# Block norms with an integer guess and Newton steps, and one memory pool per operand of gate and up, in a one-core decoder step

## The chip, the cores and the metric

The kernel is written for one NeuronCore of a Trainium2 chip. A core has five engines with an in-order instruction queue each: the matrix engine (PE, whose weight loads are listed apart as PEld), VectorE (DVE), ScalarE (ACT), GpSimd (POOL) and SyncE (SP), which here only issues DMAs. They share an on-chip memory of 128 partitions (SBUF), and matrix results go to a small accumulator memory (PSUM). The metric is the device time of one launch in microseconds; lower is better. Before the change it was 1488.21 us, the median of three runs (1481.99, 1488.21 and 1488.89).

## What is computed

One layer of a decoder with hybrid attention is applied to 1024 prompt tokens and 64 sample tokens (8 sequences of 8), 1088 columns in all, with shared weights and a width of 1024, followed by a last norm:

```python
def rms_norm(x, g):
    y = x * lax.rsqrt(jnp.mean(x * x, axis=-1, keepdims=True) + EPS)
    return y * g

h = rms_norm(x, norm_mix)
z = h @ w_in                        # queries, three K/V pairs, gates, pooling channels
o_att = nsa(...)                    # compressed, selected and window branch, gated per head
o_pool, _ = pool_mix(...)           # trailing means over 2/4/8/16 positions, small matrix each
x = x + jnp.concatenate([o_att, o_pool], axis=-1) @ w_out
h = rms_norm(x, norm_ffn)           # the "block norms" of this document
gate, up = jnp.split(h @ w_ffn_in, 2, axis=-1)      # 2 x 2816 columns
x = x + (silu(gate) * up) @ w_ffn_out
y = rms_norm(x, norm_final)
```

The new K/V rows, windows and pooling states are outputs too. A norm needs one reciprocal square root for each token: one number per partition when a tile holds 128 tokens.

## The kernel before

All matrix products are made from 32-bit numbers split in two parts of lower precision, hi and lo (`split`, lines 162 to 164): ACT casts the source to hi, DVE subtracts hi from the source to get lo. Three products (hi by hi, hi by lo, lo by hi) take the place of one. So nearly every operand of PE passes through one ACT and one DVE instruction first.

The work goes through these stages, in the order of the program.

- *First norm and projections* (0 to about 250 us). `norm1` takes x in three chunks of 384, 384 and 320 tokens. It transposes x (line 280), scales the copy by the norm's weights into `h1h` and `h1l` (lines 283 and 284), sums squares on ACT (line 293), calls `rstd_ops`, and spreads the root over the partitions with another transpose (line 300). The product with `w_in` runs on the unscaled columns, and its result is multiplied by the root (line 305).
- *Attention* (to about 698 us). Eight query blocks by two K/V groups by two head pairs give 32 units. The score products of the next unit (lines 918 and 919), their biases and minima on DVE (lines 924 and 939), the exponentials on ACT (line 949), the scaling by gates on POOL (line 997), the transposes of the probabilities (line 1007, copied out and split at 1015 and 1016) and the products with V (lines 1031 and 1032) are woven together by a stream written out by hand. Into it `fill` (called once for each transposed pair of blocks) threads a second, slower stream: first the sample tokens and the pooling half of the output projection, then `att_out`.
- *`att_out`* handles nine tiles of tokens in the order in which attention finishes them (0, 1, 2, 7, the samples, 6, 5, 4, 3): the attention half of the output projection (lines 1193 to 1195), the sum into x (line 1267), the square and its sum on ACT (line 1281), `rstd_ops`, the scaling of x into h (line 1283), and in `h_out` the transposes of h (line 1298) and the multiplication by the norm's weights (line 1299). All tiles but the last go to DRAM (`hdA`, `hdB`); the last one is written straight into the input blocks of the next stage.
- *Gate and up* (about 719 to 1190 us). The 1024 rows and 1088 columns of h form four blocks, hA[0], hA[1], hB[0] and hB[1], each 128 x 4 x 544 numbers. One product of two-by-two blocks is made with seven products instead of eight, named P1 to P7. Their right-hand operands are: P1 is hA[0], P2 is hA[1], P3 is hB[1], and P4 to P7 are sums and differences of blocks, made by `combos` (lines 1315 to 1327) in two pieces, columns 0 to 416 and then 416 to 544; only the second piece has columns of the last attention tile. Each operand is split into `bh…` and `bl…`, 128 x 2176 numbers each. The weights get the same treatment (`side_w`), four products ahead. `chains` runs the products in the order that `sequence` writes out: P1 and P2 of the first unit come first, then P1 of the second, then those that need the combinations. The program calls for the splits of P1 and P2 and two products, then for the rest of the last norm (`self.tail`), then for `combos`.
- *Down projection, last norm* (to the end), with a square root on ACT for each last norm (line 245).

Two things set the order in which instructions stand in an engine's queue. A planner places them at build time: by the order of the program, by when their inputs are expected, and with the threads of `fill` in front. And memory: a tile belongs to a pool, pools are opened and closed like a stack, and the first use of a new pool waits until all tiles under its area have had their last use. The left side of the stack holds constants, then biases (`bias`), then K and V (`kv`), and above them what the threads need, at last `wa`, the pool of `att_out` with its weights, x, h and transposed h. At the entry of gate and up (`ffn`, from line 1466) all but the constants are closed; `fs` (split weights) and then `b2` (the seven operands, some 122 KB of each partition) open over the same area. The input blocks `blk` and the raw weights `wr` lie on the right side.

ACT evaluates functions from a table held in the engine, and an instruction ACT_TABLE_LOAD stands in its queue wherever the next function needs another table. Copies, casts and squares need none of their own here.

Of the kernel before, what the change touches and what calls it, by code (L numbers as in the profile page):

```python
# [11 lines left out]
F32R = mybir.dt.float32r  # L12
I32 = mybir.dt.int32
AF = mybir.ActivationFunctionType
OP = mybir.AluOpType
# [4 lines left out]
D = 1024  # L20
# [11 lines left out]
HT = NT // 2  # L32
# [6 lines left out]
EPS = 1e-6  # L39
# [35 lines left out]
class K:  # L75
# [98 lines left out]
    def consts(self):  # L174
        nc, I, cst = self.nc, self.I, self.cst
        with ExitStack() as s:
            ip = self.pool("ii", 1, stack=s)
            ii = ip.tile([128, 128], I32, name="ii")
            nc.gpsimd.iota(ii, pattern=[[1, 128]], base=0, channel_multiplier=-1)
            self.ident = cst.tile([128, 128], F32, name="ident")  # L180
            nc.vector.tensor_scalar(self.ident, ii, 0.0, None, op0=OP.is_equal)
        self.gm = cst.tile([128, 8], F32, name="gm")
        self.gf = cst.tile([128, 8], F32, name="gf")
        self.rows = cst.tile([128, 64], F32, name="rows")
        self.psc = cst.tile([128, 4], F32, name="psc")
        self.ones = cst.tile([128, 128], F32, name="ones")
        self.ptrow = cst.tile([1, 32], I32, name="ptrow")
        nc.vector.memset(self.ones, 1.0)
        warm = cst.tile([128, 1], F32, name="warm")
        nc.scalar.activation(warm, self.ones[:, 0:1], AF.Ln)  # L190
# [50 lines left out]
    def rstd_ops(self, v, r, t, ss, root=False):  # L241
        nc = self.nc
        nc.vector.tensor_scalar(v, ss, 1.0 / D, EPS, op0=OP.mult, op1=OP.add)
        if root:
            nc.scalar.sqrt(t, v)
            nc.vector.reciprocal(r, t)
        else:
            nc.scalar.activation(t, v, AF.Ln)
            nc.scalar.activation(r, t, AF.Exp, scale=-0.5)
# [3 lines left out]
        nc.vector.tensor_tensor(r, r, t, op=OP.mult)  # L253

# [977 lines left out]
    def att_out(self, pool):  # L1232
# [19 lines left out]
        while todo or nxt:  # L1252
# [29 lines left out]
            self.rstd_ops(v[:rows], r[:rows], t[:rows], ss[:rows])  # L1282
# [186 lines left out]
    def ffn(self, att):  # L1469
        nc, I = self.nc, self.I  # L1470
        with ExitStack() as s:
# [25 lines left out]
            b2p = self.pool("b2", 1, stack=b2)  # L1497
            new = lambda q: (b2p.tile([128, 4, HT], F32R, name="bh" + q), b2p.tile([128, 4, HT], F32R, name="bl" + q))
            B.update({q: new(q) for q in ("P1", "P2", "P5", "P6", "P7", "P4", "P3")})
# [80 lines left out]
    def last_group(self, f0, acts, s):  # L1580
# [72 lines left out]
        self.rstd_ops(v, r, t, ss[:, 0:2], True)  # L1653
# [11 lines left out]
    def final_tile(self, fp, pf, gB, j):  # L1665
# [16 lines left out]
        self.rstd_ops(v[:rows], r[:rows], t[:rows], ss[:rows], True)  # L1682
# [38 lines left out]
```

## Time and profile before

| | |
|---|---|
| runs, median of three | 1488.21 us |
| profiled execution, its own time | 1487.72 us |
| its span | 1485.9 us |
| mean granted clock of PE | 0.964 |
| PE busy | 1374.0 us, 92% |
| DVE busy | 972.8 us, 65% |
| ACT busy | 691.6 us, 47% |
| POOL busy | 199.8 us, 13% |

The profile is one execution, recorded by the hardware. A page gives the busy time of each engine, then the span in 40 equal slices with the busy share in tenths; a line PEclk gives the clock that PE was granted, in tenths of full speed. A busy PE at half clock gets half the work done. Groups of instructions are named by source line, engine, operation and tile, with a count, the busy time and the mean duration in ns; behind them stands how long the engine sat idle just before and what released it, marked "<-". In the timeline each line has a start and a duration in us. Windows list, for a stretch of time, its length, the busy time of PE, PEld, DVE, ACT and POOL with the number of instructions, and then PE's clock, the share of the DMA engines and GB/s. The names there are those of the program without buffer numbers: `bhP` and `blP` are the split operands of gate and up, `blk` their source blocks.

### The profile page before, as it was taken

How to read it: one execution, taken by the hardware profiler on the slowest of the kernel's cores; microseconds unless marked ns; L12 is line 12 of the kernel's file. 1: busy time of each engine (PE TensorE's matmuls, PEld its weight loads, DVE VectorE, ACT ScalarE, POOL GpSimd, SP SyncE). 2: the span in 40 equal slices, each digit the busy share in tenths (PEclk: the TensorE clock that was granted, in tenths of full speed). 3: DMA queues.
4: the chain of work that ended last, by engine and by line, in shares of the span. 5: the costliest groups of instructions: out<-in, count | busy, mean ns of one | idle time of the engine just before them, and what ended most of it. 6: DMA issues, size and time to landing. Idle time of an engine off the chain costs nothing.

```text
span 1485.9 us, 25408 instructions
## 1 busy us (share of the span) xinstructions
PE 1374.0 (92%) x9490; PEld 1275.1 (86%) x9490; DVE 972.8 (65%) x2210; ACT 691.6 (47%) x1545; POOL 199.8 (13%) x338
## 2 busy tenths in 40 slices
PE   6979999999999988987599999999999979999996
PEld 5878999777888867766589999999999979999995
DVE  4655877787676775665775655565555555879558
ACT  7322454766565676865633333333333343525123
POOL 0114223432222221111000000000000010101000
PEclk9989999999999999988789999999999989999998
DMA  6457431543525232311523333332333251536135
GB/s 184 89 136 225 121 95 34 179 144 104 180 90 157 71 114 93 100 57 61 159 58 117 118 104 111 110 102 74 102 104 118 74 209 56 188 99 211 45 106 179
DMA packets 167751, 173.79 MB, mean 117 GB/s; under 512 B 21539, under 2 KB 134787, under 8 KB 166851
## 3 DMA queue, kind: packets, MB, share of 16 engines
q1 hardware_dynamic: 157187, 135.12, 29.8%
q0 software_dynamic: 9392, 35.45, 6.9%
q10 hardware_dynamic: 1048, 1.59, 0.9%
q8 instruction: 75, 1.23, 0.3%
q14 instruction: 49, 0.40, 0.1%
HBM read 113.87 MB, written 58.37 MB: 116 GB/s over the span
## 4 chain that ended last, share of the span: by engine, by line
PE 56%; issue 9%; DVE 8%; ACT 6%; DMA 3%; POOL 1%; SPq 0%; DVEq 0%; POOLq 0%; ACTq 0%
PE pq L1391 34%; PE tp L1007 3%; PE dp L1193 2%; PE O L1031 2%; PE dp L1194 2%; PE dp L1195 2%; PE O L1032 2%; PE S L918 2%; PE S L919 1%; DMA r<-td 1%; ACT ph L1015 1%; DVE pl L1016 1%; DVE blP L164 1%; PE dp L1150 1%; PE dp L1605 1%
## 5 line engine op out<-in xcount | busy, mean ns | idle before, releaser
L1391 PE MATMUL pq<-bhP,sh 128*128 128x272 f32 x1232 | 357.8, 291 | 8.4 <-ACT bhP L163 6.7
L1391 PE MATMUL pq<-blP,sh 128*128 128x272 f32 x1232 | 358.1, 291 | 4.4 <-DVE blP L164 4.4
L1391 PE MATMUL pq<-bhP,sl 128*128 128x272 f32 x1232 | 355.9, 289 | 0.0
L1391 PEld LDWEIGHTS pq<-bhP,sh 128*128 128x128 f32 x1232 | 234.7, 191 | 10.2 <-ACT bhP L163 8.0
L1391 PEld LDWEIGHTS pq<-blP,sh 128*128 128x128 f32 x1232 | 234.3, 190 | 5.4 <-DVE blP L164 5.4
L1391 PEld LDWEIGHTS pq<-bhP,sl 128*128 128x128 f32 x1232 | 234.5, 190 | 0.0
L1391 PE MATMUL pq<-r,sh 128*128 128x272 f32 x1008 | 194.9, 293 | 14.0 <-ACT r L1563 7.4
L163 ACT CAST sh<-ws 128x512 fp32r<-128x512 f32 (+1 forms) x136 | 78.9, 583 | 219.7 <-PE pq L1391 151.9
L1391 PEld LDWEIGHTS pq<-r,sh 128*128 128x128 f32 x1008 | 160.8, 192 | 16.0 <-ACT r L1563 7.6
L164 DVE TENSOR_TENSOR sl<-ws,sh 128x512 fp32r<-128x512 f32 (+1 forms) x136 | 86.7, 640 | 124.8 <-ACT sh L163 124.5
L1391 PE MATMUL pq<-r,sl 128*128 128x272 f32 x504 | 145.3, 289 | 0.0
L1016 DVE TENSOR_TENSOR pl<-tp,ph 128x512 fp32r<-128x512 f32 (+8 forms) x168 | 103.8, 622 | 48.4 <-ACT ph L1015 47.0
L163 ACT CAST sh<-wr 128x512 fp32r<-128x512 f32 (+1 forms) x102 | 59.3, 583 | 154.1 <-PE pq L1391 144.8
L1015 ACT CAST ph<-tp 128x512 fp32r<-128x512 f32 (+8 forms) x168 | 88.6, 533 | 74.8 <-PE tp L1007 66.5
L236 PE MATMUL dp<-h1h,whi 128*128 128x384 f32 (+1 forms) x336 | 113.9, 340 | 3.5 <-DVE ue L305 3.2
L236 PE MATMUL dp<-h1l,whi 128*128 128x384 f32 (+1 forms) x336 | 112.9, 336 | 0.2 <-DVE h1l L284 0.2
L236 PE MATMUL dp<-h1h,wlo 128*128 128x384 f32 (+1 forms) x336 | 112.9, 336 | 0.1
L1560 POOL DMA_DIRECT2D r<-td x21 | 16.0, 764 | 639.8 <-PE pq L1391 638.3
L1391 PEld LDWEIGHTS pq<-r,sl 128*128 128x128 f32 x504 | 96.6, 192 | 0.0
L164 DVE TENSOR_TENSOR sl<-wr,sh 128x512 fp32r<-128x512 f32 (+1 forms) x102 | 64.9, 637 | 39.3 <-ACT sh L163 39.2
L1031 PE MATMUL O<-ph,vn 128*128 128x256 f32 x264 | 81.7, 323 | 5.1 <-ACT ph L1015 3.8
L997 POOL TENSOR_SCALAR pwin<-pwin,r 128x640 f32<-128x640 f32 (+4 forms) x64 | 42.6, 669 | 316.5 <-DVE r L990 171.3
(348 smaller groups left out, 3108.5 us busy)
## 6 DMA issues: line engine op xcount, KB each, us to landing
wr<-in_w_ffn_in SPq DMA_DIRECT2D x44, 512.0 KB
td<-blk SPq DMA_DIRECT2D x18, 1088.0 KB
r<-td POOLq DMA_DIRECT2D x21, 816.0 KB, 6.7
wr<-in_w_ffn_out SPq DMA_DIRECT2D x48, 192.0 KB
wraw<-in_w_in SPq DMA_DIRECT2D x14, 512.0 KB
x<-in_x_prompt SPq DMA_DIRECT2D x8, 512.0 KB
qi<-qd SPq DMA_DIRECT2D x8, 512.0 KB
op<-odp SPq DMA_DIRECT2D x16, 256.0 KB
```

Source lines behind the costliest of these rows:

```text
L163: nc.scalar.copy(hi, src)
L164: nc.vector.tensor_tensor(lo, src, hi.bitcast(F32), op=OP.subtract)
L236: nc.tensor.matmul(ps, w[:, k, :], x, start=(k == 0 and j == 0), stop=(k == kt - 1 and j == 2))
L918: nc.tensor.matmul(S[:, c0:c0 + n], q, kh[:, k0:k0 + n], start=True, stop=False)
L997: nc.gpsimd.tensor_scalar(t, t, r[:, hh, b:b + 1], 1.0, op0=OP.mult, op1=OP.mult)
L1007: nc.tensor.transpose(tp[:kk, 256 * x + 128 * hh:256 * x + 128 * hh + 128], u["P"][hh, b][:, kb * 128:kb * 128 + kk], self.ident)
L1015: nc.scalar.copy(ph[:kk, a:e], tp[:kk, a:e])
L1016: nc.vector.tensor_tensor(pl[:kk, a:e], tp[:kk, a:e], ph[:kk, a:e].bitcast(F32), op=OP.subtract)
L1031: nc.tensor.matmul(o, vv, ph[:kk, cs], start=(2 * t + x == 0), stop=False)
L1032: nc.tensor.matmul(o, vv, pl[:kk, cs], start=False, stop=(2 * t + x == nb - 1))
L1193: nc.tensor.matmul(ps[:rows], oh[:, k, :rows], wh[:, k, cs], start=(k == 0), stop=False)
L1391: nc.tensor.matmul(ps[:, c, :HQ], w[:, k], x[:, k, cs], start=(fresh and k == 0 and j == 0), stop=(k == kt - 1 and j == 2), skip_group_che ...
```

## The change

There are two parts.

The norms of the first stage keep a routine that uses ACT, but with the square root in place of logarithm and exponential (`rstd_ops`, lines 241 to 253 before). The norms in `att_out` call a new routine, `rstd_bits`. It halves the bit pattern of the number, read as an integer, and subtracts it from a constant, which gives a first guess of the reciprocal root; three Newton steps of three instructions each follow, all on DVE. The warm-up instruction at the start asks for the square root's table instead of the logarithm's.

The seven operands of gate and up get one pool each, `bP1` to `bP3`, opened one after the other in the order P1, P2, P6, P5, P7, P4, P3.

```diff
--- before.py
+++ after.py
@@ -187,7 +187,7 @@
         self.ptrow = cst.tile([1, 32], I32, name="ptrow")
         nc.vector.memset(self.ones, 1.0)
         warm = cst.tile([128, 1], F32, name="warm")
-        nc.scalar.activation(warm, self.ones[:, 0:1], AF.Ln)
+        nc.scalar.sqrt(warm, self.ones[:, 0:1])
 
     def late_consts(self):
         nc, I, bp = self.nc, self.I, self.btp
@@ -238,19 +238,24 @@
                 if cnt % every == 0:
                     yield
 
-    def rstd_ops(self, v, r, t, ss, root=False):
+    def rstd_ops(self, v, r, t, ss):
         nc = self.nc
         nc.vector.tensor_scalar(v, ss, 1.0 / D, EPS, op0=OP.mult, op1=OP.add)
-        if root:
-            nc.scalar.sqrt(t, v)
-            nc.vector.reciprocal(r, t)
-        else:
-            nc.scalar.activation(t, v, AF.Ln)
-            nc.scalar.activation(r, t, AF.Exp, scale=-0.5)
+        nc.scalar.sqrt(t, v)
+        nc.vector.reciprocal(r, t)
         nc.vector.tensor_tensor(t, r, r, op=OP.mult)
         nc.vector.tensor_tensor(t, t, v, op=OP.mult)
         nc.vector.tensor_scalar(t, t, -0.5, 1.5, op0=OP.mult, op1=OP.add)
         nc.vector.tensor_tensor(r, r, t, op=OP.mult)
+
+    def rstd_bits(self, v, r, t, ss):
+        nc = self.nc
+        nc.vector.tensor_scalar(v, ss, 1.0 / D, EPS, op0=OP.mult, op1=OP.add)
+        nc.vector.tensor_scalar(r.bitcast(I32), v.bitcast(I32), -0.5, float(0x5f3759df), op0=OP.mult, op1=OP.add)
+        for _ in range(3):
+            nc.vector.scalar_tensor_tensor(t, r, v, r, op0=OP.mult, op1=OP.mult)
+            nc.vector.tensor_scalar(t, t, -0.5, 1.5, op0=OP.mult, op1=OP.add)
+            nc.vector.tensor_tensor(r, r, t, op=OP.mult)
 
     def x_src(self, j):
         if j < 8:
@@ -1279,7 +1284,7 @@
             r = pool.tile([128, 1], F32, name="r", bufs=2)
             t = pool.tile([128, 1], F32, name="t", bufs=2)
             nc.scalar.activation(h[:rows], x[:rows], AF.Square, accum_out=ss[:rows])
-            self.rstd_ops(v[:rows], r[:rows], t[:rows], ss[:rows])
+            self.rstd_bits(v[:rows], r[:rows], t[:rows], ss[:rows])
             nc.scalar.activation(h[:rows], x[:rows], AF.Copy, scale=r[:rows])
             self.tail = self.h_out(pool, j, rows, h)
             yield
@@ -1494,9 +1499,9 @@
             self.qfree = [0, 1, 2, 3]
             self.fs = self.pool("fs", 1, stack=s)
             b2 = ExitStack()
-            b2p = self.pool("b2", 1, stack=b2)
-            new = lambda q: (b2p.tile([128, 4, HT], F32R, name="bh" + q), b2p.tile([128, 4, HT], F32R, name="bl" + q))
-            B.update({q: new(q) for q in ("P1", "P2", "P5", "P6", "P7", "P4", "P3")})
+            for q in ORDER:
+                bq = self.pool("b" + q, 1, stack=b2)
+                B[q] = (bq.tile([128, 4, HT], F32R, name="bh" + q), bq.tile([128, 4, HT], F32R, name="bl" + q))
             self.ca = self.pool("ca", 1, stack=b2)
             self.split(*B["P1"], hA[0])
             self.split(*B["P2"], hA[1])
@@ -1650,7 +1655,7 @@
                 half(0, (0, 1, 2, 3))
         half(1, (4, 5, 6, 7))
         nc.vector.tensor_tensor(ss[:, 0:2], ss[:, 0:2], ss[:, 2:4], op=OP.add)
-        self.rstd_ops(v, r, t, ss[:, 0:2], True)
+        self.rstd_ops(v, r, t, ss[:, 0:2])
         for j in range(2):
             for hf in range(2):
                 cs = slice(512 * hf, 512 * hf + 512)
@@ -1679,7 +1684,7 @@
         t = fp.tile([128, 1], F32, name="ft", bufs=2)
         nc.vector.tensor_tensor(y[:rows], ps[:rows], y[:rows], op=OP.add)
         nc.scalar.activation(sq[:rows], y[:rows], AF.Square, accum_out=ss[:rows])
-        self.rstd_ops(v[:rows], r[:rows], t[:rows], ss[:rows], True)
+        self.rstd_ops(v[:rows], r[:rows], t[:rows], ss[:rows])
         nc.vector.scalar_tensor_tensor(y[:rows], y[:rows], r[:rows], gB[:rows], op0=OP.mult, op1=OP.mult)
         if b < 8:
             nc.sync.dma_start(O["y_prompt"][0, 128 * b:128 * b + 128, :], y[:rows])
```

## The prediction, made before the result was known

> **What bounds the kernel now.** I read the page first: the busy share and the granted clock of the matrix engine, slice by slice (40 slices of 37 us).
>
> ```profile
> span 1485.9 us, 25408 instructions
> ...
> PE   6979999999999988987599999999999979999996
> ...
> PEclk9989999999999999988789999999999989999998
> ```
>
> The matrix engine (PE) sets the time nearly everywhere. Only three places in reach of this change are short of nines or of clock: the start, slices 14 to 18 (attention with the block norms woven in), and slices 18 and 19, where gate and up begin. The loads of ScalarE's function tables come next, from the groups by line with shapes kept apart; columns are count, busy us and mean ns.
>
> ```profile
> L248 ACT ACT_TABLE_LOAD x11 | 14.1, 1283 | 0.2
> ...
> L249 ACT ACT_TABLE_LOAD x9 | 11.5, 1283 | 0.2
> ...
> L949 ACT ACT_TABLE_LOAD x3 | 3.8, 1283 | 0.1
> L190 ACT ACT_TABLE_LOAD x1 | 1.3, 1283 | 0.7 <-PEq L1704 0.7
> ```
>
> Twelve norms (three at the start, nine in attention) each take a logarithm (L248) and an exponential (L249), and each switches tables twice. Three of the second loads show up under the softmax (L949), because a softmax exponential came first. Then eight stretches, one around each of the first eight attention norms: length, busy us of PE, PE's weight loads, DVE, ACT and POOL, and after them PE's granted clock.
>
> ```profile
> 548.00:556.00 8.00, 6.61 (x30) 4.57 (x29) 5.00 (x18) 5.60 (x16) 0.00 (x0) 0.85 0.24 79
> 564.00:576.00 12.00, 9.24 (x47) 7.73 (x46) 5.54 (x20) 6.86 (x15) 1.85 (x3) 0.86 0.33 101
> 584.00:592.00 8.00, 5.35 (x26) 4.39 (x25) 2.36 (x10) 5.29 (x10) 1.85 (x3) 0.79 0.14 33
> 600.00:604.00 4.00, 1.89 (x11) 1.52 (x11) 2.16 (x11) 3.97 (x13) 0.00 (x0) 1.00 0.04 10
> 616.00:620.00 4.00, 2.72 (x17) 1.98 (x17) 3.45 (x12) 3.27 (x10) 0.00 (x0) 1.00 0.11 11
> 632.00:644.00 12.00, 9.84 (x37) 7.03 (x36) 6.50 (x23) 5.42 (x16) 1.63 (x3) 0.72 0.14 44
> 648.00:656.00 8.00, 5.35 (x26) 4.31 (x25) 4.40 (x21) 7.05 (x17) 1.63 (x3) 0.79 0.33 100
> 672.00:684.00 12.00, 8.21 (x41) 6.74 (x39) 5.73 (x29) 9.15 (x22) 3.26 (x6) 0.72 0.12 46
> sum 68.00, PE 49.21 PEld 38.28 DVE 35.14 ACT 46.62 POOL 10.23; mean PE 6.15 PEld 4.78 DVE 4.39 ACT 5.83 POOL 1.28
> ```
>
> PE idles 68.0 − 49.2 = 18.8 us in them, and the clock is low: length times (1 − clock), summed over the eight rows, is 13.0 us. So at most 31.8 us are at stake here. DVE is busy only half of the time (35.1 of 68).
>
> **The change part by part.** *The norms.* One norm before, and the four Newton instructions of another, from the timeline (start, us, engine, line):
>
> ```profile
> 583.77 1.28 ACT L248 ACT_TABLE_LOAD   x1
> ...
> 585.29 1.28 ACT L249 ACT_TABLE_LOAD   x1
> ...
> 586.82 0.16 DVE L250 TENSOR_TENSOR t<-r 128x1 f32<-128x1 f32 x1 [2.85 <-ACT r L249]
> ...
> 588.16 1.16 ACT L1283 ACTIVATE h<-xr,r 128x1024 f32<-128x1024 f32 x1
> ...
> 601.65 0.16 DVE L250 TENSOR_TENSOR t<-r 128x1 f32<-128x1 f32 x1 [1.85 <-ACT r L249]
> ...
> 603.91 0.15 DVE L253 TENSOR_TENSOR r<-r,t 128x1 f32<-128x1 f32 x1
> ```
>
> A load with its activation takes 1.52 us (583.77 to 585.29), so a block norm holds ACT for 3.04 us, and every cast and softmax queued behind it; DVE, whose queue is in order, stops at L250 (2.85 us). The change removes that: 24 loads here (11 + 9 + 3 + 1). It keeps one at the start (the warm-up becomes a square root) and adds one for the first exponential of the gates, so 22 loads of 1.283 us, 28 us of ACT, go. For each of the nine block norms in attention DVE runs eleven dependent instructions in place of five (the three norms at the start are costed below). The integer guess and the scalar_tensor_tensor on 128x1 do not occur before. The nearest rows are the 0.15 and 0.16 us above, and I take 0.2 us with the gap. Back to back that is 2.2 us. But DVE weaves other work between dependent instructions: four of them span 2.4 us in the second group, and eleven at that spacing take some 6.6 us. These are the two ends; six more instructions of 0.2 us for each of eight norms, 10 us of DVE, fit its idle half.
>
> The Trainium skill, "ScalarE: Activation LUTs", "Table sets: the hidden batching unit", says that one set holds logarithm and exponential, so that a pair would need one load; here each pair loads both times, and by the rule there would have been almost nothing to remove. Its section "What ACT_TABLE_LOAD costs" adds 1.38 us of draining to each load; this trace shows 1.52 us with the activation, and 22 loads would be 59 us by the page.
>
> *What of it sets the end.* PE's waits from 540 to 700 (us in total, times, longest):
>
> ```profile
> PE tp L1298 <- ACT h L1283: 6.3, 4, 2.8
> PE tp L1007 <- DVE t L251: 3.5, 1, 3.5
> ```
>
> The transposes of h (L1298) wait 6.3 us for the norm itself. A chain of 11 woven instructions is no shorter than what it replaces, so I leave these 6.3. The other 12.5 us of idle come from work queued behind the loads on ACT, or behind L250 on DVE, as in the second row. What is late next is the chain itself and DVE's evictions: I take two thirds as gained, 8.4 us. The clock:
>
> ```profile
> 588.00:592.00 4.00, 3.94 (x15) 3.26 (x16) 1.25 (x7) 1.33 (x2) 1.85 (x3) 0.60 0.27 66
> 692.00:696.00 4.00, 3.25 (x17) 2.82 (x16) 1.98 (x3) 1.74 (x4) 0.28 (x2) 0.70 0.00 0
> ```
>
> PE is full at clock 0.60 right after the stall of 584 to 588. I let the 13.0 us shrink with the idle, 13.0 x 8.4 / 18.8 = 5.8. Attention: **14.2 us**, ends 0 and 31.8. The second row is a low clock with no norm near, and it speaks against this step (below).
>
> *The start.* PE's waits up to 60 us, one load, one Newton end, the stretch after, and a reciprocal of the softmax:
>
> ```profile
> PE tp L300 <- DVE n1r L253: 2.9, 1, 2.9
> PE tp L280 <- DVE h1l L284: 2.1, 1, 2.1
> ...
> 8.98 1.28 ACT L249 ACT_TABLE_LOAD   x1
> ...
> 29.03 0.16 DVE L253 TENSOR_TENSOR n1r<-n1r,n1t 128x3 f32<-128x3 f32 x1
> ...
> 30.00:35.00 5.00, 5.00 (x22) 3.96 (x20) 2.10 (x5) 3.07 (x7) 0.00 (x0) 0.66 0.02 5
> ...
> L987 DVE RECIPROCAL r<-l 128x3 f32<-128x3 f32 x40 | 6.9, 172 | 2.3 <-ACT pwin L949 1.6
> ```
>
> These three norms do not get the guess: they take one square root on ACT, whose table the warm-up has loaded, and one reciprocal on DVE (0.17 us) in place of logarithm and exponential, and keep the Newton step. The second chunk's transposes of the root (L300) wait 2.9 us for a result that ends at 29.2 behind two loads. Without them, at 1.28 us each, it is there 2.6 us earlier; the activation that goes pays for the reciprocal that comes. So this wait goes but for some 0.3 us, which I neglect; with it half of the 1.7 us (5 x 0.34) that the low clock costs after. The load at 8.98 stands ahead of the first copies of h1, for which PE waits 2.1: 1.28 gained. Together 2.9 + 0.85 + 1.28 = **5.0 us**, ends 0 and 6.7 (2.9 + 2.1 + 1.7). The new exponential load at the gates costs 0 to 1.28; I take 0.6. The final norms keep their square root and their load.
>
> *The pools.* The seven operands of gate and up lay in one pool; now each has its own. The rows where attention ends:
>
> ```profile
> 702.03 0.97 SPq L1482 DMA_DIRECT2D blk<-hdA  x2
> ...
> 710.35 0.15 DVE L243 TENSOR_SCALAR v<-ss 128x1 f32<-128x1 f32 x1 [1.22 <-ACT h L1281]
> 713.37 0.16 DVE L250 TENSOR_TENSOR t<-r 128x1 f32<-128x1 f32 x1 [2.87 <-ACT r L249]
> 716.57 0.69 DVE L1299 TENSOR_TENSOR blk<-tp,gf 128x512 f32<-128x512 f32 x1 [2.46 <-PE tp L1298]
> 717.39 3.91 ACT L163 CAST bhP<-blk 128x2176 fp32r<-128x2176 f32 x2 [1.07 <-PE tp L1298]
> 720.78 4.75 DVE L164 TENSOR_TENSOR blP<-blk,bhP 128x2176 fp32r<-128x2176 f32 x2
> 729.00 0.69 DVE L164 TENSOR_TENSOR sl<-wr,sh 128x512 fp32r<-128x512 f32 x1 [1.67 <-ACT sh L163]
> 729.61 1.88 DVE L1318 TENSOR_TENSOR blk<-blk 128x1664 f32<-128x1664 f32 x1
> ```
>
> The casts of P1 and P2 wait for the last norm's transposes, though their data (hdA, asked for at 702.03) has nothing to do with them. No row shows when it lands; I take it as there by the time x is summed, 709.1. The one pool overlies the tiles that the transposes still read. P1 and P2 in pools at the bottom overlie only the bias and the keys, which are done. From 709.1 (the last sum of x) to the first combination at 729.61 DVE works 12.3 us and idles 1.22 + 2.87 + 2.46 + 1.67 = 8.2. With the 4.75 us of splits free to fill the gaps, and six more small instructions, 13.5 us of work are left; with 2 us of idle it starts 15.5 us after 709.1, at 724.6: **5.0 us**, ends −1.2 (the six instructions, nothing moved, or data that lands late) and 7.0 (no idle). What the casts are moved past: on ACT the last square and scaling (L1281, L1283), which would stand behind casts of 2 us each; on DVE L1267. No store, load or SP entry changes place. The last norm feeds only the second piece of the combinations, so a delay of 2 to 4 us there is covered by the first piece; without that cover it would cost its length.
>
> **The sum.** 14.2 + 5.0 + 5.0 − 0.6 = 23.6. The profiled execution took 1487.7 us (span 1485.9 and 1.8 around it), the runs have a median of 1488.2 (1482.0 to 1488.9). 1487.7 − 23.6 = **1464**.
>
> **The rivals.**
> - *The stalls come back on other engines.* The 6.3 us on h grow as the chain is woven into DVE's evictions. Attention 5, start 3, entry 1.5, less 0.6: 1479. For it: the spacing of 0.6 us above. Against: ACT is free meanwhile. Chance 0.18.
> - *The clock does not follow the stalls.* It is low at 692 to 696 without a norm; if transposes and short waits keep it so, the 5.8 and the start's 0.85 stay: 1470.6, say 1471. Chance 0.12. The Trainium skill, "TensorE: Matmul & The Clock Gate", "HAM oscillation — how this bites in real kernels", puts the limit at gaps of some 3.4 us, and the gap of 584 to 588 is under that; the row of 588 to 592 at 0.60 does not agree.
> - *Nearly everything is gained.* Start 6.7, four fifths of 31.8 = 25.4, entry 7: 1487.7 − 39.1 + 0.6 = 1449. For it: nearly all PE idle of the stretch lies at the norms. Chance 0.16.
> - *Nothing shows*, or the guess and the pools do not do what they say (the casts stay behind the transposes, the stalls keep another cause): 1481 to 1495. Chance 0.07.
> - *Slower: the woven chain.* If a PSUM eviction of 0.62 us stands between every two of the eleven, the chain takes 11 x (0.16 + 0.62) = 8.6 us where loads, activations and Newton took from 583.77 to 588.16, 4.4 us, and later with their own weaving some 6. h is 2.6 us late or more, eight times, 21 to 34 us, and POOL's scaling behind DVE's softmax sums with it; less 9.4 at start and entry: about 1500 to 1512. It decides from some 0.55 us an instruction on. Chance 0.05.
>
> **How the numbers follow.** My forecast has 0.42; its own range is 1456 to 1472. What a measurement of this kernel can tell from no change is about 0.5%, 7.4 us: below 1480.8 is faster. Faster: 0.42 + 0.12 + 0.16 and three quarters of 0.18 = 0.83; within: 0.07 and the rest of the 0.18 = 0.12; slower: 0.05. For 8 in 10 the range takes in the stalls that come back and most of the full gain: 1447 to 1482.
>
> **What would show it.** Two table loads before 540, none from 540 to 730; PE's clock near 0.95 in attention; under 10 us of idle around the norms; the casts of P1 and P2 ahead of the last transposes; combinations starting some 15 us after the last sum of x; gate and up from there on unchanged in length. I am wrong if the eleven instructions take over 6 us from first to last and PE's wait for h grows, or if the first casts still end their wait at L1298.

## The result and the profile after

The changed kernel takes 1446.84 us, the median of four runs (1445.03 to 1448.49), against 1488.55 us for the kernel before, four runs on the same chip (1481.99 to 1489.60). The ratio is 0.9728, with a 95% interval of 0.9703 to 0.9754. The forecast was 1464 us, range 1447 to 1482. The direction was right; the gain is 41.7 us and not 24, and the time lies at the very edge of the range: it is 1447 only when rounded.

From the page of the changed kernel: the span, and by slices the busy share of the matrix engine and its granted clock (40 slices of 36 us).

```profile
span 1446.7 us, 25436 instructions
...
PE   7979999899999989996799999999999989999995
...
PEclk9989999989999999998899999999999999999998
```

Counted from 0, slices 14 to 17 have one eight left of three, and their clock is in the nines. What is left is in slices 18 and 19, the entry of gate and up. ScalarE's table loads, from the groups by line with shapes kept apart:

```profile
L190 ACT ACT_TABLE_LOAD x1 | 1.3, 1283 | 0.7 <-PEq L1709 0.7
L478 ACT ACT_TABLE_LOAD x1 | 1.3, 1283 | 0.0
L1427 ACT ACT_TABLE_LOAD x1 | 1.3, 1283 | 0.0
L244 ACT ACT_TABLE_LOAD x1 | 1.3, 1283 | 0.0
```

Four loads stand where there were 26; none falls in attention. The start: the waits of PE up to 60 us (total, times, longest).

```profile
PE tp L285 <- DMA x<-in_x_prompt: 6.7, 3, 4.5
PE tp L285 <- DVE h1l L289: 0.8, 1, 0.8
```

The window from 30 to 35 us of the same kernel:

```profile
30.00:35.00 5.00, 5.00 (x33) 4.48 (x32) 3.34 (x9) 2.25 (x5) 0.00 (x0) 1.00 0.26 64
```

The wait for the root (2.9 us) is gone, the one for h1 is 0.8 instead of 2.1, and the window from 30 to 35 has the full clock and 33 matrix instructions instead of 22. Attention as a whole, from the first block norm's square to the last product with the values; first the window of the kernel before:

```profile
544.50:698.00 153.50, 131.45 (x710) 105.32 (x709) 96.30 (x320) 106.75 (x262) 29.71 (x51) 0.90 0.24 76
```

Then the same stretch of the changed kernel:

```profile
538.90:665.00 126.10, 120.42 (x711) 96.65 (x710) 101.97 (x369) 84.17 (x230) 30.34 (x51) 0.99 0.29 93
```

And PE's waits in it:

```profile
PE tp L1012 <- DVE pl L1021: 1.9, 3, 1.2
PE O L1036 <- DVE of L1047: 1.2, 1, 1.2
PE S L923 <- ACT psel L954: 1.1, 2, 0.6
PE dp L1198 <- DVE xr L1272: 0.5, 1, 0.5
PE tp L1012 <- POOL pwin L1002: 0.3, 1, 0.3
```

The same work (710 and 711 matrix instructions) takes 27.4 us less. PE's idle time falls from 153.50 − 131.45 = 22.1 us to 5.7, and its busy time falls by 11.0, because the clock rises from 0.90 to 0.99. ACT is busy for 22.6 us less; DVE for 5.7 us more. No wait for h is left.

Where the 39.2 us between the two spans lie, from the times of the same instructions in both traces:

| stretch | before | after | gain |
|---|---|---|---|
| start to the first scaled projection result | 43.5 | 35.6 | 7.9 |
| from there to the first block norm's square | 501.0 | 503.3 | −2.3 |
| attention, to the last product with the values | 153.5 | 126.1 | 27.4 |
| from there to the first product of gate and up | 21.5 | 16.0 | 5.5 |
| gate and up, first to last product | 482.2 | 484.4 | −2.2 |
| from there to the first product of the down projection | 7.9 | 4.7 | 3.2 |
| the rest | 276.3 | 276.6 | −0.3 |

Gate and up ends at 1201.7 us in the kernel before and at 1165.4 in the changed one; the 1190 given above for its end is some 12 us too early. The end of the combinations is the better mark for the entry: from the last product with the values to the last combination it was 52.7 us and is 49.5, a gain of 3.2.

### The profile page after: what moved, and what is told of

Read it like the earlier page. It is cut to its first block, busy times and chain, and to the rows that moved or that the text cites. A ratio compares the mean times of both kernels' runs of the same rounds, so it can differ in the third digit from the quotient of the medians.

```text
span 1446.7 us, 25436 instructions
## 1 busy us (share of the span) xinstructions
PE 1358.5 (94%) x9490; PEld 1263.1 (87%) x9490; DVE 980.2 (68%) x2267; ACT 660.4 (46%) x1502; POOL 200.0 (14%) x338
## 4 chain that ended last, share of the span: by engine, by line
PE 66%; issue 11%; DVE 9%; DMA 5%; ACT 4%; SPq 3%; POOL 1%; DVEq 0%; POOLq 0%; ACTq 0%
PE pq L1396 36%; PE dp L236 6%; PE tp L1012 3%; SPq L1060 3%; PE O L1036 2%; PE dp L1198 2%; PE dp L1200 2%; PE dp L1199 2%; PE O L1037 2%; PE S L923 2%; PE S L924 1%; DVE pl L1021 1%; DMA r<-td 1%; ACT ph L1020 1%; PE dp L1155 1%
```

## The experiments

The theory at test was that of the prediction with its sizes corrected: table loads hold up ACT's queue, PE starves behind it and loses its clock; the start and the pools add gains of their own. The rivals were that DVE's chain or the planner's order, not the loads, sets attention's time, and that the pools do nothing beyond the first casts. All kernels below ran beside the kernel before. The same changed kernel, run again in the second group, took 1445.64 us (1442.33 to 1449.66, ratio 0.9720, interval 0.9692 to 0.9749); single kernels are compared with the 1446 us of these two. The groups ran on different chips, so the ratio to the kernel before on the same chip is given each time.

> The changed kernel once more, on the chip of these runs, as the measure for differences of 3 us: 1445 to 1449.

**The two halves of the change.** The changed kernel with the one pool for the seven operands put back:

```diff
-            for q in ORDER:
-                bq = self.pool("b" + q, 1, stack=b2)
...
+            b2p = self.pool("b2", 1, stack=b2)
...
+            B.update({q: new(q) for q in ("P1", "P2", "P5", "P6", "P7", "P4", "P3")})
```

> The changed kernel with the seven operands of gate and up back in one pool, so the norms' part alone. If the pools gave what the two traces show at the entry of gate and up (3.1 us) and at the start of the down projection (3.3 us), this is 6.4 us above the changed kernel's 1446.8: 1453, and PE's wait there for the down projection's first operand is back at some 7 us. Rival: the pools gave nothing, and the two places moved because the last norm of attention is shorter: 1447 to 1449.

And the kernel before with the seven pools alone (the same edit the other way round):

> The kernel before with one pool per operand of gate and up, its logarithms and exponentials kept, so the pools' part alone. If the two parts add: 1488.5 - 6.4 = 1482, nothing changed before 698 us. If the pools' gain needs the short last norm: 1486 to 1489.

The norms alone took 1452.31 us (ratio 0.9777, 0.9756 to 0.9798): 34.7 us below its kernel before at 1486.97, so the pools bring 5.5 to 6.7 us on top by the medians, and 7 to 8 by the ratios. The pools alone took 1477.03 us (0.9948, 0.9929 to 0.9967), a gain of 7.7 us by the ratio and 9.9 by the medians, and faster than either expectation. From the last product with the values to the last combination it takes 47.2 us (52.7 before), and between the last product of gate and up and the first of the down projection 5.2 us (7.9 before). Its attention has the same order as the kernel before, engine by engine, by names and shapes of the instructions. It has the waits of the kernel before, the same rows with the same numbers for h, t and xr, and yet lasts 146.5 us and not 153.5:

```profile
546.90:693.40 146.50, 124.22 (x710) 100.03 (x710) 96.28 (x320) 106.46 (x262) 29.57 (x51) 0.95 0.25 80
```

Its waits of PE there, the two rows that the prediction showed of the kernel before:

```profile
PE tp L1298 <- ACT h L1283: 6.3, 4, 2.8
PE tp L1007 <- DVE t L251: 3.5, 1, 3.5
```

PE's idle time in it is 22.3 us, as before (22.1). Only the clock differs, 0.95 against 0.90. So some 7 us of attention's 27 vary with the clock of the one execution that was profiled, and idle time is the steadier measure; it is used below. The order of the changed kernel's attention, which six more of the kernels share, shows no such spread: 125.1 to 127.4 us in seven profiles.

**Loads put back, nobody waiting for them.** Logarithm and exponential of a constant for each block norm, written to a tile that nobody reads; the norm itself stays on DVE:

```diff
+            d = pool.tile([128, 2], F32, name="d", bufs=2)
+            nc.scalar.activation(d[:, 0:1], self.ones[:, 0:1], AF.Ln)
+            nc.scalar.activation(d[:, 1:2], self.ones[:, 0:1], AF.Exp, scale=-0.5)
             self.rstd_bits(v[:rows], r[:rows], t[:rows], ss[:rows])
```

> The changed kernel with two short ScalarE instructions added in each of the nine block norms, a logarithm and an exponential of a constant that nobody reads, so that each norm has its two table loads again while the root still comes from VectorE. Theory that the loads hold ScalarE's queue: most of attention's 27.5 us comes back, 1467 to 1474, with 18 loads in attention, PE idle around them and its clock near 0.9 there. Rival, that the norm's own latency or its place in the queues was what PE waited for: below 1453, clock near 0.99.

It took 1471.98 us (0.9907, 0.9884 to 0.9930), 26 us more than the changed kernel. But the planner was free to place instructions without inputs, and put all nine pairs in one row: 18 loads between 508.5 and 536 us. PE's waits from 500 to 540 us:

```profile
PE O L1036 <- ACT ph L1020: 11.7, 1, 11.7
PE tp L1012 <- DVE pl L1021: 9.0, 1, 9.0
```

The window of the same 40 us:

```profile
500.00:540.00 40.00, 18.46 (x107) 15.53 (x107) 12.72 (x44) 37.33 (x68) 3.93 (x6) 0.68 0.11 40
```

This shows directly that loads in ACT's queue stop PE through the casts of the probabilities behind them: 18 x 1.52 = 27.4 us of ACT, 26 us of time. Attention itself, from the first square on, was 126.0 us, as in the changed kernel: the time came out as expected, but not where it was expected. The run doesn't show what the loads cost where the norms stand. So the logarithm was given the sum of squares, and the exponential the logarithm's result:

```diff
...
+            nc.scalar.activation(d[:rows, 0:1], ss[:rows], AF.Ln)
+            nc.scalar.activation(d[:rows, 1:2], d[:rows, 0:1], AF.Exp, scale=-0.5)
             self.rstd_bits(v[:rows], r[:rows], t[:rows], ss[:rows])
```

> The changed kernel with a logarithm of the sum of squares and an exponential of its result added behind each block norm's square, read by nobody. Unlike the constants of the run before, they can not be moved ahead, so the 18 table loads stand where they stood before the change, on ScalarE alone; the root stays on VectorE, which waits for no ScalarE result in it. If it is ScalarE's queue that the loads held: attention again some 18 to 27 us longer than in the changed kernel, 1464 to 1474, with PE's clock near 0.9. If it was VectorE's queue, which stood at the first Newton instruction until the exponential was there: 1447 to 1453.

It took 1468.94 us (0.9863, 0.9830 to 0.9896). Its loads, from the groups by line:

```profile
L1288 ACT ACT_TABLE_LOAD x9 | 11.5, 1283 | 0.2
L1289 ACT ACT_TABLE_LOAD x7 | 9.0, 1283 | 0.1
L954 ACT ACT_TABLE_LOAD x2 | 2.6, 1283 | 0.0
```

The window of its attention:

```profile
537.40:684.70 147.30, 130.19 (x711) 105.39 (x710) 103.11 (x368) 106.91 (x262) 29.58 (x51) 0.90 0.25 79
```

And PE's longest waits in it:

```profile
PE O L1036 <- ACT ph L1020: 4.2, 3, 2.4
PE dp L1198 <- DVE xr L1272: 4.0, 2, 2.9
PE S L923 <- ACT psel L954: 3.5, 4, 1.6
```

With the loads back and nobody using what is computed behind them, the time was 22 to 23 us longer by the medians, attention had 21 of its 27 us back, and PE idled 17.1 us in it. DVE's stop at the first Newton instruction isn't needed for that, since the root here waits for nothing on ACT. That looked like a proof that the loads were the cost.

**The same number of loads, of other functions.** Three more kernels were made to question it. In the first, the block norms take the root on ACT and the reciprocal on DVE, like the norms of the start:

```diff
-            self.rstd_bits(v[:rows], r[:rows], t[:rows], ss[:rows])
+            self.rstd_ops(v[:rows], r[:rows], t[:rows], ss[:rows])
```

> The changed kernel, in which the nine block norms of attention take the square root on ScalarE and the reciprocal on VectorE, as the norms of the start do, so that each norm needs a table load for the root and the next softmax one for the exponential; neither guess nor long Newton chain. Theory A, the loads are what was costly, whoever needs them: like the two unread activations in place (1468.9), within 4 us of it: 1464 to 1473, attention from the first Square to the last product with the values 143 to 151 us. Theory B, the loads cost little where the result is waited for by nobody but the norm, and the shorter VectorE work pays: 1448 to 1458, attention 128 to 136. Theory C, a norm that waits for its own load is worse than one beside it: over 1475, attention over 153.

It took 1452.77 us (0.9770, 0.9742 to 0.9798): only 7 us more than the changed kernel, although each norm loads the root's table and the next softmax the exponential's. The next two kernels ask what made the difference to the 1468.94 us. One puts the second load back into the norm, by an exponential that nobody reads:

```diff
             self.rstd_ops(v[:rows], r[:rows], t[:rows], ss[:rows])
...
+            nc.scalar.activation(d[:rows], v[:rows], AF.Exp, scale=-0.5)
```

> The kernel with the block norms' square root on ScalarE and reciprocal on VectorE, and behind the root an exponential of the mean square into a tile that nobody reads, so that the load of the exponential's table again stands in the norm, ahead of the scaling, and not at the next softmax. As many loads in attention as there (18). Theory A, a second load inside the norm is what made the kernel before and the two unread activations in place so slow (attention 153.5 and 147.3 us against 134.1): 1462 to 1472, attention 143 to 151. Theory B, the place of the second load matters little, and the orders of the work that the planner made are what differs: 1450 to 1458, attention 131 to 138.

The other keeps guess and Newton steps, and beside them takes a root that nobody reads:

```diff
...
+            nc.scalar.sqrt(d[:rows], ss[:rows])
             self.rstd_bits(v[:rows], r[:rows], t[:rows], ss[:rows])
```

> The changed kernel with guess and Newton steps, and beside them a square root of the sum of squares on ScalarE into a tile that nobody reads: one load in the norm, the other at the next softmax exponential, 18 loads in attention, and VectorE's long chain is kept. Theory A, the loads in these places cost the 7 us that the root on ScalarE cost, and VectorE's chain costs nothing: 1450 to 1456, attention 131 to 137. Theory B, loads on ScalarE and the longer chain on VectorE hinder each other, which is why the two unread activations in place cost 23 us: 1462 to 1471, attention 142 to 150.

They took 1453.65 us (0.9818, 0.9775 to 0.9860) and 1454.54 us (0.9800, 0.9765 to 0.9836). Their group's runs of the kernel before had a median of 1484.84, so by the ratios they lie 11 to 14 us above the changed kernel, and by the medians 8 to 9. So DVE's long chain doesn't explain the slow one. The loads of these kernels in the groups by line, and the windows of their attention; first the root on ACT:

```profile
L244 ACT ACT_TABLE_LOAD x10 | 12.8, 1283 | 0.2
L954 ACT ACT_TABLE_LOAD x8 | 10.3, 1283 | 0.1
```

Its window of attention:

```profile
535.60:669.70 134.10, 124.69 (x711) 100.11 (x710) 99.33 (x328) 105.38 (x254) 29.93 (x51) 0.95 0.27 87
```

PE's longest wait in it:

```profile
PE S L923 <- ACT psel L954: 5.8, 3, 3.0
```

Root, then an exponential that nobody reads (the root's row is as above, x10):

```profile
L1289 ACT ACT_TABLE_LOAD x9 | 11.5, 1283 | 0.2
```

Its window of attention:

```profile
537.60:669.70 132.10, 121.22 (x709) 96.61 (x709) 98.10 (x328) 106.28 (x262) 30.12 (x51) 0.99 0.27 89
```

Guess and Newton steps, beside them a root that nobody reads (nine loads at the root, L1288, and eight at the softmax, L954). Its window of attention:

```profile
542.80:678.40 135.60, 125.84 (x710) 101.34 (x709) 105.51 (x368) 105.79 (x254) 29.80 (x51) 0.94 0.27 86
```

ACT is busy for 105 to 107 us in all of them, as in the kernel before, but PE's idle differs. The stretch of attention holds eight norms, and 16 of the 17 or 18 loads; the ninth norm follows at the entry of gate and up.

| kernel | loads in attention | attention, us | PE idle, us | clock |
|---|---|---|---|---|
| before | 16 | 153.5 | 22.1 | 0.90 |
| pools alone | 16 | 146.5 | 22.3 | 0.95 |
| logarithm, then exponential of it, unread | 16 | 147.3 | 17.1 | 0.90 |
| root, then exponential of another tile, unread | 16 | 132.1 | 10.9 | 0.99 |
| root on ACT | 16 | 134.1 | 9.4 | 0.95 |
| root, unread | 16 | 135.6 | 9.8 | 0.94 |
| six Newton steps (next experiment) | 0 | 131.2 | 10.7 | 0.97 |
| changed, two profiles | 0 | 126.1, 125.2 | 5.7, 6.0 | 0.99, 1.00 |

The same 16 loads go with 9.4 us of idle in one kernel and with 22.3 in another. By ACT's timelines the second load of a norm starts 1.5 to 2.0 us after the first in all six kernels (once 4.7, with the unread root): where the norm asks for no exponential, the next softmax does at once. So the kernel that was to put the second load back into the norm hardly moved it, and a second function that reads what the first has written holds ACT no longer than one that doesn't.

What loads as such cost in attention is not isolated either: the kernel with six Newton steps has none there and idles 10.7 us all the same. What ended PE's waits tells more. Waits that end at an exponential or a cast of the probabilities on ACT (`psel`, `pwin`, `ph`) come to 1.1 us in the changed kernel and 0.8 with six Newton steps, to 5.5, 6.3 and 6.6 in the three kernels with a root on ACT, and to 9.5 with the unread logarithm. So some 5 us of idle go with the loads in those three kernels; their attention is 6 to 10 us longer than in the changed kernel, and their time 7 to 14.

The other 6 to 13 us of idle in the slower kernels are not explained by the loads. The kernel before and the one with the pools alone share an order of instructions in attention; each of the other kernels with loads there has an order of its own, since the planner makes it anew, and that order alone may be what differs. A kernel with the order of the kernel before held fixed, and the loads alone taken out, was not tried. What of the 27 us belongs to the loads and what to the order stays open.

**DVE's chain.** Six Newton steps instead of three, nine more instructions a norm:

```diff
-        for _ in range(3):
+        for _ in range(6):
```

> The changed kernel with six Newton steps in place of three: 20 dependent VectorE instructions for each block norm, nine more at 0.2 us, woven into other work, so h comes some 4 to 5 us later. If only ScalarE's queue mattered and the order of the queues takes the longer chain into account: 1446 to 1451. If the chain of the norm is on the path, as the slower rival of the prediction has it: nine norms by 4 to 5 us less what is covered, 1465 to 1490.

It took 1451.51 us (0.9783, 0.9757 to 0.9809), 5 to 6 us more by the medians, 8 to 9 by the ratios, for 81 instructions; this is just above the first of the two expectations. From the end of the square to the start of the scaling a norm now takes 10.0 us in the mean of nine, where it took 6.0 (and 5.7 in the kernel before). PE's wait for it, from the waits from 535.5 to 666.7 us:

```profile
PE tp L1303 <- ACT h L1288: 1.6, 2, 1.3
```

A norm that is 4 us longer makes PE wait 1.6 us for h in all. But that is not its whole price, as the window of attention shows:

```profile
535.50:666.70 131.20, 120.53 (x710) 97.49 (x709) 113.03 (x440) 84.79 (x230) 29.66 (x51) 0.97 0.28 89
```

PE idles 10.7 us, about 5 more than in the changed kernel, and most of the rest ends at other instructions of DVE and POOL. How much of it is the work on DVE, 11 us more, and how much the new order, no run tells apart.

**The start.** The changed kernel with the three norms of the start and the warm-up back on logarithm and exponential:

```diff
-        nc.scalar.sqrt(warm, self.ones[:, 0:1])
+        nc.scalar.activation(warm, self.ones[:, 0:1], AF.Ln)
...
+            nc.scalar.activation(t, v, AF.Ln)
+            nc.scalar.activation(r, t, AF.Exp, scale=-0.5)
...
-            self.rstd_ops(v, r, t, ss)
+            self.rstd_ops(v, r, t, ss, True)
```

> The changed kernel, in which the three norms of the start and the warm-up go back to logarithm and exponential; attention and pools stay as changed. Theory A, the start is a gain of its own that the rest doesn't give back: its traces differ by 7.9 us at the first product of the first stage after the start (43.5 before, 35.6 after), while the stages up to the first block norm gave back 2 us in one profile and nothing in another: 1445.6 + 6 to 8, so 1451 to 1454, with the matrix engine's clock low from 30 to 35 us and a wait of 2 to 3 us on n1r. Theory B, what the start saves is lost again on loads of the first weights, so that only about 2 us of it reach the end: 1446 to 1449, with the first block Square at 537 or earlier although the start is late. My prediction's term was 5.0: 1450.6.

It took 1453.71 us (0.9772, 0.9747 to 0.9797), 7 to 8 us more. The start is a gain of its own, and it reaches the end. In this profile the first scaled result comes at 46.1 us, 10.5 after that of the changed kernel and 2.6 after that of the kernel before, with the clock low for longer. PE's waits up to 60 us:

```profile
PE tp L309 <- DVE n1r L253: 2.9, 1, 2.9
PE tp L289 <- DVE h1l L293: 2.1, 1, 2.1
```

The windows that follow:

```profile
30.00:35.00 5.00, 5.00 (x21) 4.01 (x19) 2.09 (x5) 3.09 (x7) 0.00 (x0) 0.59 0.02 5
35.00:40.00 5.00, 5.00 (x18) 3.12 (x16) 1.10 (x2) 4.23 (x7) 0.00 (x0) 0.50 0.00 0
40.00:45.00 5.00, 5.00 (x20) 5.00 (x20) 2.70 (x7) 1.47 (x3) 0.00 (x0) 0.55 0.33 89
```

**The pools, taken apart.** P1 and P2 with a pool each, the other five in one:

```diff
-            for q in ORDER:
+            for q in ("P1", "P2"):
...
+            bq = self.pool("brest", 1, stack=b2)
+            for q in ORDER[2:]:
```

> The changed kernel with pools of their own for P1 and P2 alone and one pool for the other five operands. Theory that a new pool waits for the whole of every pool that it overlies: the entry of gate and up stays as in the changed kernel (some 49.5 us from the last product of attention to the last combination), but the loads of the down projection's first operands wait for the last product again, 7.9 us from the last product of gate and up to the first of the down projection in place of 4.7: 3 us slower than the changed kernel. Rival, that tiles are released one by one: no difference.

It took 1451.35 us (0.9752, 0.9724 to 0.9780), 4 to 6 us more. The entry was kept (49.5 us from the last product with the values to the last combination), but the gap ahead of the down projection was 8.0 us again. PE's waits there, in the changed kernel first:

```profile
PE pq L1396 <- ACT r L1568: 4.2, 1, 4.2
```

The DMAs of the ring in the same kernel, from POOL's timeline:

```profile
1163.26 5.40 POOL L1565 DMA_DIRECT2D r<-td  x7 [502.84 <-PE pq L1396]
```

The same DMAs in the kernel before:

```profile
1202.49 5.38 POOL L1560 DMA_DIRECT2D r<-td  x7 [510.21 <-PE pq L1391]
```

And PE's wait with the five operands in one pool:

```profile
PE pq L1396 <- ACT r L1571: 7.5, 1, 7.5
```

The down projection reads its ring of operands `r` back from DRAM through seven DMAs on POOL, and the ring overlies the operands of gate and up. In the changed kernel the DMAs are issued at 1163.26, 2 us ahead of the last product of gate and up (1165.4); in the kernel before they were issued at 1202.49, after it (1201.7). If the ring waits for what it overlies, a ring of seven pools should be faster still:

```diff
-            ring = self.pool("ring", 1, stack=s4)
+            ring = [self.pool(f"ring{j}", 1, stack=s4) for j in range(7)]
...
-                r = ring.tile([128, 2, kt, HT], F32R, name=f"r{nr[0] % 7}")
+                r = ring[nr[0] % 7].tile([128, 2, kt, HT], F32R, name=f"r{nr[0] % 7}")
```

> The changed kernel with one pool for each of the seven buffers of the down projection's operands in place of one pool for all seven. By the same theory the first buffers wait only for P1 and P2 of the last unit and not for P4, so their loads are asked for some 10 us earlier and PE's wait of 4.7 us between the two projections falls to 1 or less: 3 to 6 us faster than the changed kernel, 1441 to 1444. Rival, that the loads are held by the DMA queue or by their data: no difference.

It took 1440.62 us (1435.67 to 1442.41, ratio 0.9671, 0.9642 to 0.9700), 5.0 us below the changed kernel on the same chip, and faster than both kernels of this case. The two intervals overlap a little (0.9692 to 0.9700). The DMAs of its ring, from POOL's timeline:

```profile
1139.10 0.84 POOL L1565 DMA_DIRECT2D r<-td  x1 [480.37 <-PE pq L1396]
1148.12 0.76 POOL L1565 DMA_DIRECT2D r<-td  x1 [8.19 <-PE pq L1396]
...
1165.15 0.76 POOL L1565 DMA_DIRECT2D r<-td  x1 [7.25 <-PE pq L1396]
```

They start 24 us earlier and nearly one by one, and PE waits for `r` no more. The planner also moved the work: the first product of the down projection (1156.7) now stands 10.6 us ahead of the last of gate and up, so that the gain is that of the pools and the new order together.

## Why the prediction was right in direction and short in size

- *The loads.* Twenty-two fewer, none in attention: as said. That they hold ACT's queue and what stands behind it is shown by the 18 loads in one row. That they are the main cost of the norms, as the prediction took it, is not shown: in the three kernels with a root on ACT, some 5 us of idle and 7 to 14 us of time go with them, of attention's 20 to 27 us, and each of these kernels has another order too.
- *"A chain of 11 woven instructions is no shorter than what it replaces, so I leave these 6.3."* This step failed. The first half was right: the norm takes 6.0 us where it took 5.7. But PE's wait for h went from 6.3 us to nothing. PE's wait doesn't follow the norm's length: at 10.0 us a norm it is 1.6 us. So the wait can't be the norm's length alone; it came with the order of that kernel's work, and a wait that another order can remove can't be left in the sum on the ground that its chain is as long.
- *"I take two thirds as gained, 8.4 us."* Mis-sized: PE's idle in attention fell by 16.4 us. (Two thirds of 12.5 are 8.3; this changes nothing.)
- *The clock, 5.8 of 13.0 us.* Mis-sized for the same reason: PE's busy time fell by 11.0 us. In proportion to the idle that is gone, as the step had it, some three quarters of the loss would go; the clock of 0.99 says nearly all did. By the two profiles of one order, 0.90 and 0.95, part of this is chance. Attention is 27.4 us by the two profiles, where the term was 14.2 with an upper end of 31.8.
- *The chain's price.* Right. In the norm that follows, the first of attention, the guess starts at 540.84 and the last Newton step at 545.65 (timeline of DVE):

```profile
540.53 0.14 DVE L253 TENSOR_SCALAR v<-ss 128x1 f32<-128x1 f32 x1
...
540.84 0.15 DVE L254 TENSOR_SCALAR r<-v 128x1 int32<-128x1 int32 x1
...
541.24 0.21 DVE L256 SCALAR_TENSOR_TENSOR t<-r,v 128x1 f32<-128x1 f32 x1
...
545.65 0.15 DVE L258 TENSOR_TENSOR r<-r,t 128x1 f32<-128x1 f32 x1
```

  From first to last that is 5.3 us, where 6.6 were reckoned; over the nine norms it is 2.5 to 7.0, and 5.3 in the mean. The unknown instructions took 0.15 and 0.21 us here, where 0.2 was taken with the gap; the second takes 0.28 in the mean of 24 (L256).
- *The start, 5.0 us, upper end 6.7.* Mis-sized: 7.9 by the profiles, 7 to 8 by the kernel that undoes it. The two waits went as said (2.9 and 1.3). The low clock went whole (1.7 us, of which half was counted). The rest, 2.0 us, was in no term: up to the first scaled result PE is busy for 28.0 us, where it was 31.6 − 1.7 = 29.9 with as many instructions.
- *The entry, 5.0 us.* The mechanism was right, the size too large: 3.2 us. The timeline of the changed kernel:

```profile
668.95 0.97 SPq L1487 DMA_DIRECT2D blk<-hdA  x2
...
675.37 0.69 DVE L1272 TENSOR_TENSOR xr<-dp,xr 128x512 f32<-128x512 f32 x1 [3.15 <-PE dp L1200]
675.46 2.00 ACT L163 CAST bhP<-blk 128x2176 fp32r<-128x2176 f32 x1 [7.86 <-DMA blk<-hdA]
...
687.73 1.89 DVE L1323 TENSOR_TENSOR blk<-blk 128x1664 f32<-128x1664 f32 x1 [0.87 <-DMA blk<-hdB]
...
691.62 0.72 DVE L1426 TENSOR_TENSOR g<-pq,g 128x544 f32<-128x544 f32 x1 [2.00 <-PE pq L1396]
```

  The first cast now waits for its data and for no transpose, and the data lands as x is summed, as assumed. The first combination starts 11.7 us after the last sum of x, earlier than the 15.5 reckoned. But the second starts only at 695.86, 8.1 us after the first, where it had followed after 2.4 (732.05 after 729.61, with one eviction between them that didn't wait). The planner put between them an eviction that waits for PE (L1426), two multiplications of the last norm (L1304) and splits of weights. The step took the order behind the first combination as given. In the kernel with the pools alone the second follows after 1.9 us (717.54 after 715.61), and the entry is 5.5 us shorter: there the term came out, so that its size, too, hangs on the order.
- *"Gate and up from there on unchanged in length."* Nearly (482.2 and 484.4), but behind it 3.2 us were gained that no term held. The prediction looked at what the pools release at their opening, and not at what they release when they close: the ring of the down projection.
- *The exponential's load at the gates, 0.6 us.* The load is there (L478); no run shows its price apart.
- *The rivals.* The one that came nearest was "nearly everything is gained", 1449, at 0.16. Its terms were 6.7, 25.4 and 7; 7.9, 27.4 and 3.2 were measured, with 3.2 more at the down projection. That the clock would not follow is refuted (0.99). The slower woven chain didn't come: the instructions are some 0.5 us apart in the norm above, near the 0.55 from which that rival was to decide, but its price was wrong, since nine instructions more a norm, and 4 us, cost 5 to 9 us, where 2.6 us a norm were priced at 21.
- *The test the prediction named for itself.* "Under 10 us of idle around the norms" came true, and so did the casts ahead of the transposes; the clock was above the 0.95 named. "None from 540 to 730" holds for the norms' loads, but not to the letter: the load of gate and up's own activation (L1427) stands at 692.49, where it was at 733.35 (L1422), since that stage begins earlier.

## What to carry to other kernels

Where a planner orders the work anew after each edit, a wait in the old trace is a property of the old order: before it is left in a sum, ask whether the waiting chain is really as long as the wait implies. Two kernels with the same number of table loads differed by 15 us in their medians and by 7 in the ratios to the kernel before, so a run that puts a suspected cost back needs a second one that puts back the same cost in another form. And where pools are opened like a stack, look at both ends: what has to be done before a pool opens, and what waits for it to close.

## What the runs showed of the hardware that was not expected

The same stall of PE was followed by different clocks. In the kernel before, a wait of 2.93 us for the root at the start is followed by 0.66 from 30 to 35 us and by 1.00 after; in the kernel with the start undone, a wait of 2.92 us at the same place is followed by 0.59, 0.50 and 0.55 over 15 us. By length times (1 − clock) that is 1.7 us against 6.8. The kernel with the pools alone, whose start has the same order, shows 0.50 from 31 to 43 us after the same wait (2.9). Attention in the same order, with equal waits, had 0.90 in one profile and 0.95 in another. A loss of clock read from one profile is thus one sample, and not a size. The Trainium skill, "TensorE: Matmul & The Clock Gate", "HAM oscillation — how this bites in real kernels", asks for gaps of PE under some 3.4 us; here a gap of 2.9 us was followed by a low clock in both profiles.

Loads of ScalarE's tables cost the same for every function here, 1283 ns, whether the root, the logarithm or the exponential was asked for. But of two kernels with 17 and 18 of them for the block norms one took 7 us more than the changed kernel and the other 23, by the medians, and which it is can't be seen from ACT's busy time in attention, 105.4 and 106.9 us. The order of the work differs between the two as well.
